# Projecting queries and keys of five heads in the first phase of an encoder layer

## The chip, the cores and the metric
The kernel runs on one core of a Trainium2 chip. The metric is the device time of one execution in microseconds (us); three runs of the kernel before gave 2012.86, 2015.05 and 2019.13 us, median 2015.05. All times below are from these runs or from one profiled execution.

## The reference
Two streams, 512 prompt frames and 64 sample frames (576 columns together, kept transposed: features on the partitions, frames along the free axis), go through two layers of width 2048. Layer A, which the change touches, is attention over chunks of 64 frames with a learned bias by relative distance:

```python
def a_project(h, w_in, g_q, g_k):
    q, k, v, g = jnp.split(h @ w_in, 4, axis=-1)
    return rmsnorm(q.reshape(hd), g_q), rmsnorm(k.reshape(hd), g_k), v.reshape(hd), g
...
sc = einsum('bqhd,bkhd->bhqk', q, kk) * A_SCALE + bias
p  = softmax(sc)
y  = x + (silu(g) * einsum('bhqk,bkhd->bqhd', p, vv)) @ w_out
```

with h = rmsnorm(x, ln), 16 heads of 128, so that `w_in` has 64 column blocks of 128: 16 of queries, 16 of keys, 16 of values, 16 of gates. Layer B is latent attention and is left as it is. All is in float32; a product is made of three matmuls on operands that are split into a high and a low part.

## The kernel before
Every operand x is split by `split` (L205, L206): ScalarE rounds it to a high part (named ...h), VectorE subtracts to get the low part (...l). `mm3` then issues high x high, high x low and low x high. A **direct projection** of one 128-wide block, `proj`, takes 16 x 3 x 2 = 96 matmuls of 288 columns. A **pair by block products**, `block_pairs`, makes two blocks together from seven products of half-size matrices, each of 24 matmuls of 288 columns: 168 in place of 192. It needs operands formed once from x (`block_operands`, tiles aiT4 to aiT7) and for every pair seven weight combinations, which `block_weights` adds on VectorE and splits (14 splits of 128 x 512, in place of 8).

PE's order is written out by the program: generators ("streams") run in `Order`, which keeps a planned time `od_.now`; a stream yields the planned time, the condition or the PSUM tag that it waits for, and the first ready stream of lowest rank issues next. The other engines' orders are set by the scheduler of the tile framework. PSUM has tags "mm" (2 buffers), "st" (1) and "x" (2).

Layer A goes in these stages:
- **First pass** (`values_and_gates`, L698): values 0, 1 and gates 0, 1 are projected together (tiles av, ag; 16 x 24 matmuls) while x is loaded. `stats_a` (tile lnast) sums the squares; from it comes `rs`, the row scale of the norm. Gates are copied out of PSUM (L716, L720); the two value results stay in the two "mm" buffers until `later` scales them by `rs` (L676) and gives "mm" back. Then value 2 and gate 2 are projected directly (tile ap) while the block operands are formed.
- **Block stage** (tiles ai35 to ai47): 13 pairs (value j, gate j), j = 3 to 15. Results go to DRAM through GpSimd's queue (`vT`, `vd`, `sgd`).
- **Heads** (`head_a`, L768): for head hd the query and key block are projected directly (tile a{hd}p). `qk_chain` copies the result out of PSUM (`raw_of`, L500), takes sums of squares (`halves`, L450 to L454, and a matmul a{hd}{0,1}st), scales (`rnorm`, L484 to L496) and splits into q and k operands. `v_chain` loads the value from `vd` (tile vt) and transposes it (vts, vtp). `attention` issues four score tiles and one for the sample (s0 to s3, s-1), transposed probabilities (t0 to t3, t-1) and the outputs (o-1, o3), in the order `ATT`; a score tile goes through softmax (L519 to L524) and back to PE as a transpose. While attention waits, PE takes matmuls of the next heads' projection: 192 per head.
- **Output projection**: the first two blocks (tile ao, `both`) run beside the last heads, as far as `heads_a` has split the heads' outputs (tiles oh, ol); block operands are formed from the outputs (L295); the rest are pairs (ao4 to ao14).

Of the kernel before, what the change touches and what calls it, by code (L numbers as in the profile page):

```python
# [20 lines left out]
P = 128  # L21
# [97 lines left out]
def encoder(tc, xT, wa_in, wa_out, wb_in, wuq, wuk, wuqr, wuv, wb_out, kcT, vc, ckvcT, krcT, gains, rtab,  # L119
# [25 lines left out]
    od = dram.tile([D, N], F32, name="od")  # L145
    vd = dram.tile([D, N], F32, name="vd")
    sgd = dram.tile([D, N], F32, name="sgd")
    qrd = dram.tile([D, N], F32, name="qrd")
    qd = dram.tile([D, N], F32, name="qd")

# [490 lines left out]

    ws = Weights(wload4, [(kt,) for kt in range(KT)], 2)
    h, xs = [], []
    state = {"ln": 0.0, "scored": -1, "in": False}

    def load_x(kt):
        x = tpx("x", F32, f"x{kt}")
# [36 lines left out]
        nc.gpsimd.dma_start(sgd[hd * P:(hd + 1) * P, :], y)  # L684

    def out_of(m, src, y):
        (value_of if m < MG else gate_a)(m, src, y)

    def y_tile(m):
        return tpy("y", F32, f"y{m}")  # L690

    def later(m, src, y, tag, n=1):
        yield lambda: state["ln"]
        out_of(m, src, y)
        if tag:
            od_.give(tag, L_M)

    def values_and_gates():  # L698
# [6 lines left out]
        for kt in range(KT):  # L705
            hi, lo = ws.get(3)
            for w in range(4):
                s = slice(w * P, (w + 1) * P)
                mm3(outs[w], (hi[:, s], lo[:, s]), [[x[:, c * 288:(c + 1) * 288] for x in h[kt]] for c in range(2)],
                    kt == 0, kt == KT - 1)  # L710
            yield None
            if kt + 4 < KT:
                load_x(kt + 4)
            square_sum(acc, xs[kt], tpx, N, kt == 0, f"lna{kt}")
        g1 = y_tile(MG + 1)
        ACT.copy(two(g1), pg1[:, :, :288])  # L716
        od_.give("st", L_M)
# [2 lines left out]
            ACT.copy(g0[:, c * 288:(c + 1) * 288], pg0[c][:, :288])  # L720
            od_.give("x", L_M)
        od_.spawn(1, stats_a(acc))
        for j in range(2):
            od_.spawn(1, later(MV + j, pv[j][:, :, :288], y_tile(MV + j), "mm"))
        od_.spawn(1, later(MG, two(g0), g0, None))
        od_.spawn(1, later(MG + 1, two(g1), g1, None))
        oX = Ahead((pair_x(j) for j in range(8)), 1)
# [8 lines left out]
        for _ in form:  # L736
# [1 line left out]
        close(g_x)  # L738
        g_w1, wp1 = pool("wblocks")
        pools.append(g_w1)  # L740
        yield from block_pairs(wa_in, X, [(MV + j, MG + j) for j in range(3, H)],
                               lambda name: wp1.tile([P, WH], F32, tag="o", bufs=10, name=name), None, y_tile,
                               lambda m, y: out_of(m, two(y), y), "ai")

# [18 lines left out]
        V.memset(t[:, :256], 0.0)  # L763
        nbA.append(t)
    o2 = [None] * H
    ws = Weights(wload, [p for hd in range(H) for w in range(2) for p in parts_of(wa_in, [w * H + hd], "wa")], 2)

    def head_a(hd):  # L768

# [2 lines left out]

        def qk_chain(which, ps):
            col = gak if which else gaq
            raw = raw_of(ps, tpa, N, f"{n_}raw{which}")
            if which:
                kc = ap_.tile([P, NC], F32, tag="kc", bufs=2, name=n_ + "kc")
                nc.sync.dma_start(kc, kcT[hd * P:(hd + 1) * P, :])
            yield lambda: state["ln"]
            st = yield from halves(raw, tpa, N, f"{n_}{which}")  # L780
            t0 = max(od_.now, state["ln"] - 2.0)
            z = rnorm(st, P, N, base=EX, coef=P * EPS / D)
            scaled(raw, col, z)
            yield lambda: state["scored"] >= hd - 1
            if which == 0:
                hi = ap_.tile([P, N], F32R, tag="qh", bufs=1, name=n_ + "qh")
                lo = ap_.tile([P, N], F32R, tag="ql", bufs=1, name=n_ + "ql")
                split(raw, hi, lo)
            else:
                nc.gpsimd.dma_start(kT[hd * P:(hd + 1) * P, :], raw)  # L790
                hi = ap_.tile([P, NK], F32R, tag="kh", bufs=1, name=n_ + "kh")
                lo = ap_.tile([P, NK], F32R, tag="kl", bufs=1, name=n_ + "kl")
                split(raw, hi[:, NC:], lo[:, NC:])
                split(kc, hi[:, :NC], lo[:, :NC])
            yield max(t0 + L_RN, od_.now + L_SP)
            got[which] = hi, lo

        def v_chain():
            vt = tpa("raw", F32, n_ + "vt")
            nc.gpsimd.dma_start(vt, vd[hd * P:(hd + 1) * P, :])  # L800
            vs = ap_.tile([P, 2, P], F32, tag="vs", bufs=2, name=n_ + "vs")
            nc.sync.dma_start(vs[:, 0, :], vc[hd * P:(hd + 1) * P, :])
# [11 lines left out]
            vl = ap_.tile([P, 512], F32R, tag="vl", bufs=1, name=n_ + "vl")  # L814
            split(tps, vh, vl)
            od_.give("x", L_T)
            got["v"] = vh, vl, vs

        sg = op_.tile([P, N], F32, tag="o", bufs=16, name=n_ + "sg")
# [2 lines left out]

        def bias():

            T = ap_.tile([P, 256], F32, tag="T", bufs=2, name=n_ + "T")
            nc.sync.dma_start(T, rtab[hd * P:(hd + 1) * P, :])
            nb = nbA[hd % 2]
            nbs = ap_.tile([P, PK], F32, tag="nbs", bufs=1, name=n_ + "nbs")
            V.tensor_scalar(out=nb[:, 256:], in0=T, scalar1=T[:, 0:1], scalar2=-1.0,
                            op0=ALU.subtract, op1=ALU.mult)  # L830
            V.tensor_copy(nbs, nb[:, 256:256 + PK])
            V.memset(nb[0:64, 448:], BIG)
            return nb, nbs
# [22 lines left out]

        od_.spawn(0, attend())
        for which in range(2):
            yield "mm"
            ps = ps_of("mm", f"{n_}p{which}")  # L860
            yield from proj(ps, ws, h, N)
            od_.spawn(1, qk_chain(which, ps))
        od_.spawn(1, v_chain())

# [471 lines left out]

L_VT, L_G, L_CQ, L_M, L_V, L_LN, L_HA, L_LB = 5.0, 5.8, 10.0, 1.5, 5.0, 5.0, 8.0, 4.0
ATT = "t0 s2 t1 s3 o-1 t2 t3"
DIRECT, GA, WRAW, WHL, SGB, DEEP, VA = 2, 2, 3, 5, 2, 2, 2
LAT = (0, 1, 2, 3, 8, 4, 5, 6, 7, 9, 10)  # L1340
LAHEAD = 1
# [85 lines left out]
```

## Time and profile before

| | |
|---|---|
| median of three runs | 2015.05 us (2012.86 to 2019.13) |
| profiled execution | 2007.77 us, its span 2005.9 us |
| TensorE (PE) busy | 1956.2 us, 98% of the span |
| VectorE (DVE) busy | 1491.2 us, 74% |
| ScalarE (ACT) busy | 1180.6 us, 59% |
| mean granted TensorE clock | 0.988 of 2.4 GHz |

Engines run at the same time, so their busy times don't add up to the span. A matmul's own duration is longer than its share of PE, since matmuls are pipelined: what one costs is the distance to the next start. "Idle before" in a row is the time that the engine stood still ahead of the instruction, with the instruction or DMA that ended it.

### The profile page before, as it was taken

What the parts mean: (1) busy time and instruction counts of PE and PEld (TensorE: products, weight loads), DVE (VectorE), ACT (ScalarE), POOL (GpSimd) and SP (SyncE); (2) the same over time, 40 slices, a digit from 0 to 9 for tenths busy, and PEclk for the clock granted to TensorE, in tenths of its full rate; (3) what the DMA queues carried; (4) which work ended last, traced back from release to release, by engine and by line L of the source; (5) the groups of instructions that cost most, each with busy time, mean ns of one, the idle gap of its engine ahead of it and who ended that gap; (6) DMA issues with size and microseconds to landing.
All of it is one profiled execution on the core that took longest, in us unless ns stands there. A gap on an engine that the chain in (4) does not pass through costs nothing.

```text
span 2005.9 us, 37809 instructions
## 1 busy us (share of the span) xinstructions
PE 1956.2 (98%) x14380; PEld 1932.3 (96%) x14380; DVE 1491.2 (74%) x2935; ACT 1180.6 (59%) x2214; POOL 136.9 (7%) x258
## 2 busy tenths in 40 slices
PE   8699999999999999999999899999999999999998
PEld 8699999999999999998999899999999999999998
DVE  8778888757777777779887648887776766776875
ACT  7655555556656565665544538986765666564332
POOL 1100000020000000000000200000000000002000
PEclk9899999999999999999999899999999999999999
DMA  7534444353222323222543525553222322256542
GB/s 232 190 117 135 141 133 134 120 198 92 91 91 88 98 81 99 84 92 66 190 148 108 182 80 147 161 165 117 78 84 88 91 86 83 83 153 222 168 143 64
DMA packets 125446, 247.00 MB, mean 123 GB/s; under 512 B 15808, under 2 KB 30160, under 8 KB 125264
## 3 DMA queue, kind: packets, MB, share of 16 engines
q1 hardware_dynamic: 104288, 171.46, 28.8%
q0 software_dynamic: 20976, 73.13, 10.5%
q8 instruction: 113, 1.85, 0.4%
q14 instruction: 69, 0.57, 0.1%
HBM read 198.07 MB, written 43.79 MB: 121 GB/s over the span
## 4 chain that ended last, share of the span: by engine, by line
PE 86%; issue 8%; DVE 2%; DMA 2%; ACT 1%; POOL 0%; SPq 0%; POOLq 0%; DVEq 0%; ACTq 0%
PE g L166 8%; PE lat L166 7%; PE u L166 4%; PE ao L166 2%; PE ap L166 1%; PE av L166 1%; PE a15p L166 1%; PE a14p L166 1%; PE a13p L166 1%; PE a12p L166 1%; PE a10p L166 1%; PE a9p L166 1%; PE a8p L166 1%; PE a7p L166 1%; PE a6p L166 1%
## 5 line engine op out<-in xcount | busy, mean ns | idle before, releaser
L206 DVE TENSOR_TENSOR wa_2l<-wa_2r,wa_2h 128x512 fp32r<-128x512 f32 x35 | 24.2, 691 | 19.7 <-ACT wa_2h L205 19.6
L205 ACT CAST wa_2h<-wa_2r 128x512 fp32r<-128x512 f32 x35 | 21.7, 620 | 21.4 <-PE a3p L166 1.9
L205 ACT CAST wa_0h<-wa_0r 128x512 fp32r<-128x512 f32 x35 | 21.5, 614 | 21.5 <-PE a0p L166 3.2
L206 DVE TENSOR_TENSOR wa_0l<-wa_0r,wa_0h 128x512 fp32r<-128x512 f32 x35 | 23.9, 684 | 11.7 <-ACT wa_0h L205 11.6
L206 DVE TENSOR_TENSOR wa_3l<-wa_3r,wa_3h 128x512 fp32r<-128x512 f32 x35 | 24.1, 687 | 11.1 <-ACT wa_3h L205 11.1
L206 DVE TENSOR_TENSOR wb_1l<-wb_1r,wb_1h 128x512 fp32r<-128x512 f32 x25 | 17.2, 688 | 15.0 <-ACT wb_1h L205 15.0
L166 PE MATMUL u<-cqh,wq_0h 128*128 128x288 f32 x128 | 27.7, 298 | 0.5 <-ACT q6raw L500 0.3
L205 ACT CAST wa_3h<-wa_3r 128x512 fp32r<-128x512 f32 x35 | 21.3, 609 | 10.4 <-PE a0p L166 4.4
L166 PE MATMUL u<-cqh,wq_0l 128*128 128x288 f32 x128 | 27.4, 296 | 0.0
L166 PE MATMUL u<-cql,wq_0h 128*128 128x288 f32 x128 | 27.3, 295 | 0.0
L206 DVE TENSOR_TENSOR wb_3l<-wb_3r,wb_3h 128x512 fp32r<-128x512 f32 x25 | 17.2, 687 | 13.2 <-ACT wb_3h L205 13.2
L166 PE MATMUL lat<-bh,wb_0h 128*128 128x288 f32 x88 | 19.9, 309 | 6.3 <-ACT bh L210 6.3
L205 ACT CAST wb_3h<-wb_3r 128x512 fp32r<-128x512 f32 x25 | 15.4, 616 | 17.8 <-PE lat L166 8.1
L205 ACT CAST wb_1h<-wb_1r 128x512 fp32r<-128x512 f32 x25 | 15.5, 618 | 17.5 <-PE lat L166 8.8
L206 DVE TENSOR_TENSOR wa_1l<-wa_1r,wa_1h 128x512 fp32r<-128x512 f32 x35 | 24.1, 689 | 2.0 <-ACT wa_1h L205 1.5
L166 PE MATMUL g<-bh,wb_1h 128*128 128x288 f32 x112 | 24.3, 298 | 0.0
L166 PE MATMUL g<-bh,wb_0h 128*128 128x288 f32 x112 | 24.3, 298 | 0.0
L166 PE MATMUL g<-bh,wb_2h 128*128 128x288 f32 x112 | 24.2, 298 | 0.0
L166 PE MATMUL g<-bh,wb_3h 128*128 128x288 f32 x112 | 24.2, 298 | 0.0
L166 PE MATMUL g<-bh,wb_0l 128*128 128x288 f32 x112 | 24.0, 296 | 0.0
L166 PE MATMUL g<-bh,wb_1l 128*128 128x288 f32 x112 | 24.0, 296 | 0.0
L166 PE MATMUL g<-bl,wb_1h 128*128 128x288 f32 x112 | 24.0, 296 | 0.0
(8217 smaller groups left out, 8616.4 us busy)
## 6 DMA issues: line engine op xcount, KB each, us to landing
wa_0r<-wa_in SPq DMA_DIRECT2D x34, 256.0 KB, 3.0
wa_1r<-wa_in SPq DMA_DIRECT2D x34, 256.0 KB, 3.1
wa_2r<-wa_in SPq DMA_DIRECT2D x34, 256.0 KB, 2.9
wa_3r<-wa_in SPq DMA_DIRECT2D x34, 256.0 KB, 3.0
wb_0r<-wb_in SPq DMA_DIRECT2D x25, 256.0 KB, 3.2
wb_1r<-wb_in SPq DMA_DIRECT2D x25, 256.0 KB, 3.2
wb_2r<-wb_in SPq DMA_DIRECT2D x25, 256.0 KB, 3.1
wb_3r<-wb_in SPq DMA_DIRECT2D x25, 256.0 KB, 2.9
```

The lines of the kernel that those rows point to most:

```text
L166: nc.tensor.matmul(out, lhs, rhs, start=start, stop=stop, **kw)
L205: ACT.copy(hi, src)
L206: V.tensor_tensor(out=lo, in0=src, in1=hi.bitcast(F32), op=ALU.subtract)
```

## The change
Heads 2, 5, 8, 11 and 14 (`EARLY`) get their query and key blocks as five more pairs at the end of the block stage. The raw results are stored to a new DRAM tensor `qkd`; `qk_chain` of these heads loads them into a tile of its own (`rawd`, two buffers) in place of copying from PSUM, and `head_a` projects nothing for them. At most two q/k chains and three raw tiles may be in work at once (`chains`, `raws`). The value tile `vt` has one buffer of its own, the bias tile `T` one in place of two. Value 0 of the first pass is copied out of PSUM by ScalarE straight after its last matmul, and its "mm" buffer is given back then.

```diff
+    qkd = dram.tile([2 * D, N], F32, name="qkd")
...
     def out_of(m, src, y):
-        (value_of if m < MG else gate_a)(m, src, y)
+        if m < MV:
+            nc.gpsimd.dma_start(qkd[m * P:(m + 1) * P, :], y)
+        else:
+            (value_of if m < MG else gate_a)(m, src, y)
...
+        v0 = y_tile(MV)
+        ACT.copy(two(v0), pv[0][:, :, :288])
+        od_.give("mm", L_M)
         g1 = y_tile(MG + 1)
...
-        for j in range(2):
-            od_.spawn(1, later(MV + j, pv[j][:, :, :288], y_tile(MV + j), "mm"))
+        od_.spawn(1, later(MV, two(v0), v0, None))
+        od_.spawn(1, later(MV + 1, pv[1][:, :, :288], y_tile(MV + 1), "mm"))
...
-        yield from block_pairs(wa_in, X, [(MV + j, MG + j) for j in range(3, H)],
+        yield from block_pairs(wa_in, X, [(MV + j, MG + j) for j in range(3, H)] + [(hd, H + hd) for hd in EARLY],
...
-    ws = Weights(wload, [p for hd in range(H) for w in range(2) for p in parts_of(wa_in, [w * H + hd], "wa")], 2)
+    ws = Weights(wload, [p for hd in range(H) if hd not in EARLY for w in range(2)
+                          for p in parts_of(wa_in, [w * H + hd], "wa")], 2)
...
-            raw = raw_of(ps, tpa, N, f"{n_}raw{which}")
+            if ps is None:
+                yield lambda: state["scored"] >= hd - 2
+                raw = ap_.tile([P, N], F32, tag="rawd", bufs=2, name=f"{n_}raw{which}")
+                r0 = (which * H + hd) * P
+                nc.gpsimd.dma_start(raw, qkd[r0:r0 + P, :])
+            else:
+                yield lambda: state["raws"] < 3
+                state["raws"] += 1
+                raw = raw_of(ps, tpa, N, f"{n_}raw{which}")
...
             yield lambda: state["ln"]
+            yield lambda: state["chains"] < 2
+            state["chains"] += 1
             st = yield from halves(raw, tpa, N, f"{n_}{which}")
...
             scaled(raw, col, z)
+            state["chains"] -= 1
...
+            if ps is not None:
+                state["raws"] -= 1
...
         def v_chain():
-            vt = tpa("raw", F32, n_ + "vt")
+            yield lambda: state["v"] >= hd - 1 and state["scored"] >= hd - 2
+            vt = ap_.tile([P, N], F32, tag="vt", bufs=1, name=n_ + "vt")
...
-            T = ap_.tile([P, 256], F32, tag="T", bufs=2, name=n_ + "T")
+            T = ap_.tile([P, 256], F32, tag="T", bufs=1, name=n_ + "T")
...
         for which in range(2):
-            yield "mm"
-            ps = ps_of("mm", f"{n_}p{which}")
-            yield from proj(ps, ws, h, N)
+            ps = None
+            if hd not in EARLY:
+                yield "mm"
+                ps = ps_of("mm", f"{n_}p{which}")
+                yield from proj(ps, ws, h, N)
             od_.spawn(1, qk_chain(which, ps))
...
+EARLY = 2, 5, 8, 11, 14
```

The change moves instructions on several engines (the changed file's lines of helpers stand one higher). Three places follow.

ScalarE at the end of the first pass, before (wa_3h is a weight split of the direct projection that comes next, aiT... block operands, xx reloaded x, y<-ag the copy of gate 1):

```order
L205 CAST wa_3h<-wa_3r 128x512
L205 CAST aiT5h_1131<-xx_1068 128x288
L205 CAST aiT7h_1141<-xx_1068 128x288
L661 ACTIVATE xx_1124<-xx_1124,gn 128x576
L205 CAST aiT6h_1137<-xx_1071 128x288
L205 CAST wa_0h<-wa_0r 128x512
L716 COPY y_761<-ag_171 128x576
```

and now (y<-av is the new copy of value 0):

```order
L206 CAST wa_3h<-wa_3r 128x512
L720 COPY y_762<-av_170 128x576
L206 CAST aiT5h_1133<-xx_1070 128x288
L662 ACTIVATE xx_1126<-xx_1126,gn 128x576
L206 CAST aiT6h_1139<-xx_1073 128x288
L206 CAST aiT7h_1143<-xx_1070 128x288
L206 CAST wa_0h<-wa_0r 128x512
L723 COPY y_764<-ag_172 128x576
```

The new copy stands right behind wa_3h, six instructions ahead of the copy of gate 1.

PE in head 14 before, ahead of the transpose of its first score tile (a15p is the projection of head 15, which fills the time since score tile 1):

```order
L166 MATMUL a15p_11123<-hh_439,wa_2l 128x288 x2
L166 MATMUL a15p_11123<-hh_479,wa_2h 128x288 x2
L166 MATMUL a15p_11123<-hl_480,wa_2h 128x288 x2
L166 MATMUL a15p_11123<-hh_479,wa_2l 128x288 x2
L166 MATMUL a15p_11123<-hh_519,wa_3h 128x288 x2
L166 MATMUL a15p_11123<-hl_520,wa_3h 128x288 x2
L166 MATMUL a15p_11123<-hh_519,wa_3l 128x288 x2
L166 MATMUL a15p_11123<-hh_559,wa_3h 128x288 x2
L166 MATMUL a15p_11123<-hl_560,wa_3h 128x288 x2
L166 MATMUL a15p_11123<-hh_559,wa_3l 128x288 x2
L170 MATMUL a14t_11272<-idt,a140P 128x128
L166 MATMUL a14s_11276<-a14kh,a14qh 128x384
```

and now, from the sample tile's transpose on:

```order
L171 MATMUL a14t-1_11682<-idt,a14sP 64x128
L167 MATMUL a14s_11688<-a14kh,a14qh 128x256
L167 MATMUL a14s_11688<-a14kl,a14qh 128x256
L167 MATMUL a14s_11688<-a14kh,a14ql 128x256
L171 MATMUL a14t_11698<-idt,a140P 128x128
L167 MATMUL a14s_11702<-a14kh,a14qh 128x384
L167 MATMUL a14s_11702<-a14kl,a14qh 128x384
L167 MATMUL a14s_11702<-a14kh,a14ql 128x384
L171 MATMUL a14t_11712<-idt,a141P 128x128 x2
L167 MATMUL a14s_11717<-a14kh,a14qh 128x512
```

The projection matmuls between score tiles and transposes are gone here: no head is left to project, and the output projection waits for heads.

DVE in head 14 now (a0sg to a13sg are finished heads' outputs, from which L296 forms block operands; L592 is the product of gate and output of head 13, the last row the softmax's first step on score tile 0):

```order
L592 TENSOR_TENSOR a13sg<-a13sg,a13o_11642 128x512
L296 TENSOR_TENSOR a10sg<-a10sg,a2sg 128x288
L296 TENSOR_TENSOR a3sg<-a3sg 128x288
L296 TENSOR_TENSOR a10sg<-a10sg 128x288
L207 TENSOR_TENSOR ol_11657<-a13sg,oh_11656 128x576
L296 TENSOR_TENSOR a3sg<-a11sg,a3sg 128x288
L296 TENSOR_TENSOR a4sg<-a4sg 128x288
L296 TENSOR_TENSOR a11sg<-a11sg,a3sg 128x288
L296 TENSOR_TENSOR a4sg<-a12sg,a4sg 128x288
L520 ISA a140P,a140sm<-a14s_11666,nbA_6173 128x128
```

Operand forming of the output stage stands between head 14's softmax steps; before, most of it stood in head 15.

## Rows read from the trace of the kernel before

**Rows 1.** Page, parts 1 and 2: busy times; PE and its clock in 40 slices.
```profile
PE 1956.2 (98%) x14380; PEld 1932.3 (96%) x14380; DVE 1491.2 (74%) x2935; ACT 1180.6 (59%) x2214; POOL 136.9 (7%) x258
...
PE   8699999999999999999999899999999999999998
...
PEclk9899999999999999999999899999999999999999
```
**Rows 2.** Timeline of PE after the first pass: start, us, instruction, idle before.
```profile
68.16 1.33 PE L166 MATMUL lnast<-lnas,ones 128*128 128x288 f32 x4 [7.86 <-ACT y L716]
...
76.81 0.85 PE L166 MATMUL ap<-hh,wa_0h 128*128 128x288 f32 x2 [7.31 <-DVE y L676]
```
**Rows 3.** Timeline of ACT at the same place.
```profile
64.63 0.60 ACT L205 CAST wa_3h<-wa_3r 128x512 fp32r<-128x512 f32 x1
...
67.48 0.63 ACT L716 COPY y<-ag 128x576 f32<-128x576 f32 x1
```
**Rows 4.** Windows by stage; columns in the first line.
```profile
core 0: us, PE busy (x) PEld busy (x) DVE busy (x) ACT busy (x) POOL busy (x), PEclk, DMA share, GB/s
60.31:76.81 16.50, 1.33 (x5) 0.99 (x5) 13.64 (x31) 12.28 (x26) 2.36 (x5) 0.59 0.53 167
76.81:104.23 27.42, 27.42 (x194) 27.42 (x195) 16.68 (x28) 10.87 (x19) 4.29 (x8) 0.94 0.59 200
329.80:352.01 22.21, 22.21 (x171) 22.21 (x170) 18.07 (x30) 12.20 (x23) 1.62 (x3) 1.00 0.42 136
...
583.44:616.26 32.82, 32.82 (x246) 32.42 (x246) 23.72 (x56) 19.99 (x42) 1.08 (x2) 1.00 0.30 91
898.50:931.14 32.64, 32.64 (x242) 31.99 (x242) 32.19 (x72) 24.10 (x50) 0.55 (x1) 1.00 0.22 67
931.14:951.48 20.34, 16.41 (x93) 13.72 (x91) 17.26 (x55) 7.84 (x22) 0.00 (x0) 0.81 0.20 61
```
**Rows 5.** Chain that ended last: start, us, pieces in head 6.
```profile
596.39 7.20 PE a6p L166 x54
```
**Rows 6.** Timeline of PE in head 1: wait for head 0's value.
```profile
426.53 0.27 PE L170 MATMUL a0vts<-idt,a0vt 128*64 128x128 f32 x1 [1.79 <-DMA a0vt<-vd]
```
**Rows 7.** Groups by line and form, DVE, heads 6 and 14: busy, mean ns, idle before.
```profile
L206 DVE TENSOR_TENSOR wa_2l<-wa_2r,wa_2h 128x512 fp32r<-128x512 f32 x2 | 1.4, 692 | 1.2 <-ACT wa_2h L205 1.2
...
L206 DVE TENSOR_TENSOR ol<-a14sg,oh 128x576 fp32r<-128x576 f32 x1 | 0.8, 751 | 0.0
```
**Rows 8.** Timeline of head 15, all engines: one softmax step.
```profile
936.30 0.28 PE L166 MATMUL a15s<-a15kh,a15ql 128*128 128x256 f32 x1
...
936.72 0.42 DVE L519 CUSTOM_DVE_ANT_0 a151P<-a15s,nbA 128x256 f32<-128x256 f32 x1
...
937.20 0.44 DVE L295 TENSOR_TENSOR a11sg<-a11sg,a3sg 128x288 f32<-128x288 f32 x1
937.56 0.44 DVE L295 TENSOR_TENSOR a4sg<-a12sg,a4sg 128x288 f32<-128x288 f32 x1
...
938.36 0.34 DVE L524 TENSOR_SCALAR a151P<-a151P,a151sm 128x256 f32<-128x256 f32 x1
```
**Rows 9.** Timeline of PE, end of head 15.
```profile
943.96 1.11 PE L170 MATMUL a15t<-idt,a153P 128*128 128x128 f32 x4 [0.41 <-DVE a153P L524]
945.75 0.80 PE L166 MATMUL a15o<-pth,a15vh 128*128 128x512 f32 x1 [0.68 <-ACT pth L205]
...
951.48 0.85 PE L166 MATMUL ao<-oh,wao_3h 128*128 128x288 f32 x2 [1.55 <-ACT oh L205]
```
**Rows 10.** DMA issues: count, KB each, median us to landing.
```profile
vd<-y POOLq DMA_DIRECT2D x16, 288.0 KB, 4.6
...
a5vt<-vd POOLq DMA_DIRECT2D x1, 288.0 KB, 3.2
```

More of the change, by code (lines that the diff above doesn't have):

```diff
@@ L643, in encoder @@
     h, xs = [], []
-    state = {"ln": 0.0, "scored": -1, "in": False}
+    state = {"ln": 0.0, "scored": -1, "in": False, "chains": 0, "raws": 0, "v": -1}
     def load_x(kt):
@@ L816, in v_chain @@
             od_.give("x", L_T)
+            state["v"] = hd
             got["v"] = vh, vl, vs
```

## The prediction
> **What bounds the kernel now.** I read the page first: PE is busy for 98% of the span, DVE for 74%, ACT for 59%, and the slices dip only at three seams [rows 1]. So time is PE's matmuls plus the places where PE stands. The windows by stage show the two stages that matter. In the heads PE is busy for all 32.82 us of a head while DVE works 23.72 [rows 4]. In the block stage a pair takes 22.21 us, all of it PE [rows 4]. The timeline of PE shows the largest wait: after the first pass it stands 7.86 us, does four matmuls, and stands 7.31 us more, until the values have been scaled and leave PSUM [rows 2].
>
> A matmul of 288 columns costs 7.20 / 54 = 0.1333 us [rows 5]. A head is then 192 x 0.1333 = 25.6 us of projection and 32.82 - 25.6 = 7.2 us of attention.
>
> **The sum is made against the profiled execution** (2007.77 us, span 2005.9) and carried over to the median of the runs, 2015.05, which is 7.3 us above it; I take the difference as the same for both kernels.
>
> **1. Five projections become five pairs.** 5 x (25.6 - 22.2) = 17.0 us off PE. The pairs I bound with the row of the present pairs: these have DVE busy 18.07 of 22.21 [rows 4], and the new ones have no gate to compute, so PE stays the limit there. Weight loads stay at eight blocks of 256 KB a head on SP's queue. On GpSimd's queue come ten stores and ten loads of 288 KB; such a store lands in about 4.6 us and such a load in 3.2 [rows 10], the loads are issued a head ahead or more, and DMA is at 0.30 in the heads: nothing. **-17.0**.
>
> **2. Value 0 leaves PSUM at once.** In ACT's order the new copy stands right behind the split of wa_3h, which ended at 64.63 + 0.60 = 65.2; with the 0.63 of such a copy [rows 3] the buffer is free at about 65.9, and the direct projection starts there instead of at 76.81 [rows 2]. The clock was at half level then as now (the window 60.31 to 76.81 has 0.59 [rows 4]), so that cost is the same. The statistic's four matmuls now come after 30 of the projection; its chain to the scaled values took 76.81 - 69.49 = 7.3 us and must end before the first of the two blocks is done, else PE waits for the second "mm" buffer. A clock of 0.94 over the 27.42 us of the projection now [rows 4] is 3.3 us at half level (0.06 / 0.5), 14 matmuls; so it reaches 30 at 65.9 + 3.3 + 16 x 0.1333 = 71.3, and the chain ends at 79 to 82 and the block at 80.8: about 1 us of wait. I take 10.9 - 1.4 = 9.5; the best is 10.6, and 6 if the chain, which shares ACT and DVE with the block operands, comes 4 us later. **-9.5**.
>
> **3. Head 0's value is loaded earlier** (its DMA now stands ahead of the gates' loads on GpSimd's queue): the 1.79 us wait goes [rows 6]. **-1.8**.
>
> **4. One buffer for vt and T.** The next value is loaded once the last was transposed. The nearest case is head 2: some 36 matmuls and a score tile, 6 us, lie between, against 3.2 us of landing [rows 10] and the issue. Nothing; at worst 2 us. A load of T holds the weight loads behind it on SP until the last bias was made, which in DVE's order lies ahead; three raw weight tiles cover it.
>
> **5. The heads lose their filler.** This is the term that decides. PE keeps 11 x 192 matmuls to fill 16 attentions. The new order spends about 150 a head in heads 2 to 10, enough to cover each wait, and has 72, 96, 96 and 12 (with the output projection's) in heads 11 to 14. From head 11's first score to head 15's first score PE needs 276 x 0.1333 + 4 x 7.2 - 2.1 (the output of head 14, which now stands behind) = 63.5 us.
>
> DVE needs more. A head's own DVE work is 23.72 less eight weight splits of 0.69 [rows 4, 7] = 18.2. In heads 11 to 14 the order has four of these less 21 rows of the q/k chains that now come earlier (0.67 each): 58.8; 11 weight splits of the output projection (7.6); 14 splits of heads' outputs at 0.75 [rows 7] (10.5); 26 forming steps at 0.45 (11.7) [rows 8]. Neighbours overlap, since two forming steps of 0.44 start 0.36 apart [rows 8]: 51 x 0.08 = 4 off. That is 84.6. The same reckoning gives head 14 of before 31.0, where the row has 32.19 [rows 4], so I go up a little, to 86. So heads 11 to 14 take 86 and not 63.5: +22.5. Head 15 in turn: it took 20.34 us with 48 filler matmuls [rows 4], that is 20.34 - 6.4 - 7.2 = 6.7 above its content; with 6 fillers every softmax step is bare. One step, from the end of the scores to P, took 936.4 to 938.7, 2.3 us [rows 8], and the last transpose to the restart of the output projection 7.5 [rows 9]. I take 8.7 above content: +2. Together **+24.5**. Below: if DVE didn't matter, four bare heads would still hold 2.3 us steps that PE can't fill, about +12. Above: if PE and DVE also wait for each other in turn, +33.
>
> The Trainium skill has a sentence that speaks against this edit ("Perfetto Trace Analysis", Matmul Optimizations): matmul speed is scaled with utilization, so matmuls should come back to back in batches. The trace agrees: granted clock 0.81 in head 15's window [rows 4], where fillers run out. By it the bare heads 14 and 15 would run their 14.4 us of attention at the 1.2 GHz level, up to 14 us more, most of it under DVE's time.
>
> **6. Heads 0 to 10** hold DVE busier: 18.2 and six weight splits (22.3 us) to 150 matmuls and 7.2 (27.2 us) is 82% instead of 72, and near 95 in heads 0 and 1, where the order has three heads' chains at once. In head 14 of before DVE was busy 32.19 of 32.64 and PE never waited [rows 4], so I take little: **+2**, 0 to 10.
>
> Sum: -17.0 - 9.5 - 1.8 + 24.5 + 2 = -1.8 us, that is 2013.2. A change of under 0.3% (6 us) can't be told from none.
>
> **The rivals.**
> *Faster: the tail is cheap.* All but terms 5 and 6 give -28.3. If DVE's extra rows slip into gaps, term 5 is near +12: -14, 2001. For it: PE did not wait in head 14 before, at 99% DVE. Against it: there 32 us of PE work covered those 32 us of DVE, and now PE's content is less than DVE's. The extreme of it follows from a rule of the Trainium skill ("Perfetto Trace Analysis", Identifying the Most-Contended Engine): performance comes from the engine of highest occupancy, to be improved first. Taken by PE's 98% alone, nothing is lost in the heads and the time is 2015.05 - 28.3 = 1986.8. The row of head 14, where DVE has 99%, says that in this stretch the engine is another. I give this extreme 0.05 of the faster chance.
>
> *Slower: the bare tail pays twice.* In heads 11 to 15 PE waits for a softmax step, DVE then waits for PE's transpose, and the granted clock falls to the half level, as its 0.81 in head 15 shows for part of that window [rows 4]; then term 5 is 33 and more, term 6 up to 10, and the sum is +15: 2030. It decides from terms 5 and 6 together above 34.3. For it: every row of the order in head 14 depends on the row before. Against it: the scheduler puts softmax ahead of other DVE work.
>
> *The copy of value 0 does nothing*, as ACT stands in front of it for a load of x, or the second buffer is awaited in full: term 2 is -3, the sum +5: no change, still within the forecast.
>
> **Chances.** With terms 5 and 6 together below 22.3 it is faster by more than 6 us, above 34.3 slower; I expect 26.5 of 12 to 43. No change 0.40, faster 0.34, slower 0.26. The likeliest case's own range is 2009 to 2021; 2000 to 2028 takes in both neighbours but for the far ends.
>
> **What would show it.** Ap starting near 66 us and ai35 near 95; five pairs of 22.2 us; heads 2 to 10 at 24 to 29 us with PE full; then heads 11 to 14 with DVE full and PE waiting for DVE rows, some 23 us in all, and clock 0.5 in heads 14 and 15. Wrong would be: PE full up to head 14, or PE waits spread over heads 0 to 10, or DVE idle in the tail.

## The result and the profile after

The changed kernel is slower: median 2041.47 us (2038.77 to 2043.47) against 2013.95 (2012.54 to 2019.13) for the kernel before; the ratio is 1.0131, with a 95% interval of 1.0109 to 1.0153. Forecast were 2013.2 us and "no change", with a range of 2000 to 2028. The profiled execution after took 2041.44 us, its span 2039.7. The profiled execution of before (2007.77) lies 6.2 us under its median, so the two spans differ by 33.8 us where the medians differ by 27.5; the account below is of the spans.

The page after, parts 1 and 2 (answering to [rows 1]):

```profile
PE 1961.4 (96%) x14260; PEld 1927.0 (94%) x14260; DVE 1538.5 (75%) x3020; ACT 1199.4 (59%) x2255; POOL 147.9 (7%) x278
...
PE   8899999999999999987999899999999999999998
...
PEclk9899999999999999988899999999999999999999
```

PE has 120 recorded matmuls fewer and yet 5 us more busy time. It has gaps in slices 18 and 19, 867 to 969 us, and slices 18 to 20 have a lower clock: they hold heads 11 to 15.

**The first pass** went nearly as forecast. PE's timeline after (start, us, instruction, idle before; compare [rows 2]):

```profile
67.03 0.85 PE L167 MATMUL ap<-hh,wa_0h 128*128 128x288 f32 x2 [7.12 <-ACT y L720]
...
73.61 0.70 PE L167 MATMUL lnast<-lnas,ones 128*128 128x288 f32 x4
...
96.01 0.29 PE L167 MATMUL ai35a<-hh,ai35p10h 128*128 128x288 f32 x1
```

The direct projection starts at 67.0 in place of 76.8, the first pair at 96.0 in place of 104.1. Then a little is given back; waits of PE in the first pass and the block stage after (line waited, what for: us, times, longest):

```profile
PE ap L167 <- ACT y L720: 7.1, 1, 7.1
PE ai35a L167 <- DVE y L414: 1.7, 1, 1.7
PE ai35a L167 <- ACT y L412: 0.6, 1, 0.6
```

The first pair stands 2.3 us for its results, which go into tiles y. There are four of these, and the copied value now holds one: VectorE, ahead of scaling value 2 into a tile y, stands until a store from such a tile has landed, where it didn't wait before (start, us, instruction, idle before):

```profile
90.08 0.76 DVE L677 TENSOR_TENSOR y<-ap,rs 128x576 f32<-128x576 f32 x1 [3.30 <-DMA vd<-y]
```

That the 2.3 us come from this wait alone is not shown. The last value pair starts at 365.6 against 370.9: 5.3 us are kept.

**The heads.** Windows after, cut at each head's first score tile s0 (heads 0, 1, 4, 8, then 11 to 15, the last up to the restart of the output projection; columns as in [rows 4]):

```profile
547.80:576.10 28.30, 28.30 (x213) 27.89 (x212) 25.07 (x60) 23.00 (x47) 1.09 (x2) 1.00 0.27 84
576.10:603.00 26.90, 25.05 (x183) 24.20 (x183) 23.26 (x57) 18.58 (x41) 1.62 (x3) 1.00 0.36 112
...
658.20:689.40 31.20, 29.01 (x204) 28.38 (x203) 26.49 (x61) 20.57 (x42) 2.70 (x5) 0.95 0.36 116
...
774.40:806.00 31.60, 29.02 (x204) 28.26 (x203) 20.28 (x50) 20.14 (x41) 0.54 (x1) 0.95 0.22 68
...
863.90:892.30 28.40, 21.85 (x132) 19.72 (x131) 22.07 (x53) 21.31 (x43) 0.54 (x1) 0.82 0.16 48
892.30:919.40 27.10, 22.40 (x150) 20.86 (x149) 25.94 (x61) 21.01 (x44) 1.08 (x2) 0.94 0.23 71
919.40:944.10 24.70, 19.81 (x137) 18.06 (x136) 23.92 (x65) 13.09 (x30) 1.63 (x3) 1.00 0.26 82
944.10:962.00 17.90, 13.10 (x55) 10.12 (x55) 12.72 (x43) 7.04 (x19) 0.71 (x1) 0.66 0.05 16
962.00:981.27 19.27, 13.55 (x54) 9.66 (x52) 10.72 (x33) 7.42 (x20) 0.00 (x0) 0.68 0.03 5
```

From head 11 on neither PE nor DVE is full, and the clock is lower in four of the five heads.

**What PE's work alone would take** can be worked out: the filler matmuls (288 columns each, of the next heads' projections and of the first output blocks) that PE takes between two first score tiles, by 0.1333 us, and 7.2 us of attention a head. This sum I call **the content**. Before, heads 0 to 10 have 2082 fillers, so 277.5 + 79.2 = 356.7 us, and heads 11 to 14 have 762, so 130.4. The two stretches of the trace of before are:

```profile
443.70:800.70 357.00, 357.00 (x2656) 352.62 (x2655) 259.95 (x604) 219.67 (x450) 11.89 (x22) 1.00 0.30 91
800.70:931.50 130.80, 130.80 (x973) 128.96 (x972) 104.56 (x239) 84.86 (x174) 3.79 (x7) 1.00 0.27 83
```

So the reckoning holds within 0.4 us. After, they have 1662 and 264 fillers: 300.7 and 64.0 us. The trace after:

```profile
547.80:863.90 316.10, 306.90 (x2238) 300.41 (x2236) 256.23 (x604) 213.29 (x443) 16.24 (x30) 0.99 0.31 96
863.90:962.00 98.10, 77.17 (x468) 68.76 (x467) 84.65 (x218) 62.44 (x134) 3.95 (x7) 0.87 0.18 57
```

What a stretch takes beyond its content I call **the loss**: 15.4 us in heads 0 to 10 and 34.1 in heads 11 to 14; before, 0.3 and 0.4. Heads 11 to 14 have 78, 96, 84 and 6 fillers and lose 10.8, 7.1, 6.2 and 10.0 us. Head 15 loses 19.3 - 7.2 - 0.8 = 11.3, before 6.4.

| part | us |
|---|---|
| first pair starts earlier, less what the block stage gave back | -5.2 |
| ten projections gone (960 x 0.1333), five pairs added (111.0) | -17.0 |
| ahead of the first score (50.6 to 48.9) | -1.7 |
| loss in heads 0 to 10 | +15.1 |
| loss in heads 11 to 14 | +33.7 |
| loss in head 15 | +4.9 |
| behind the restart of the output projection | +4.0 |
| sum (spans: 33.8) | +33.8 |

The last row is in stages that the change doesn't touch. That stretch took 1054.4 us before and 1058.4 after, but 1054.1 in run 6, which has the same early heads: it varies between executions, and I don't count it as an effect of the change. Its cause is open.

**How the tail loses.** The chain that ended last, after, at the start of head 11 (start, us, pieces):

```profile
866.29 0.42 DVE a111P L520
866.73 0.21 DVE a110P L525
...
867.07 0.30 PE a11t L171
867.37 0.54 PE a11s L167 x3
867.93 0.56 DVE a112P L520
868.50 0.28 DVE a111P L525
...
868.91 0.66 PE a11t L171 x2
...
872.62 0.53 ACT a13raw L501
...
873.20 3.25 PE a15p L167 x12
```

Within 7 us the end passes from DVE to PE, back to DVE, to PE, ACT and PE: each waits for another. PE stands from 870.85 to 873.20 while DVE and ACT are both busy; over heads 11 to 14 none of the three is busy throughout. The last row shows the second price: 12 fillers took 3.25 us, 0.27 each, where they take 0.133 at full clock [rows 5]. Windows of the same stretch, and of a wait in head 4:

```profile
655.00:660.40 5.40, 5.40 (x43) 5.20 (x41) 5.34 (x16) 3.17 (x8) 0.00 (x0) 1.00 0.01 2
660.40:662.60 2.20, 0.04 (x1) 0.01 (x1) 1.63 (x4) 2.17 (x5) 0.00 (x0) 1.00 0.35 115
662.60:664.60 2.00, 1.98 (x11) 1.95 (x11) 2.00 (x3) 0.99 (x2) 0.00 (x0) 0.63 0.45 142
664.60:666.60 2.00, 2.00 (x11) 2.00 (x10) 1.08 (x5) 1.63 (x4) 0.54 (x1) 0.52 0.29 110
666.60:668.60 2.00, 2.00 (x17) 2.00 (x17) 1.77 (x5) 1.86 (x5) 0.00 (x0) 1.00 0.10 39
...
870.85:873.20 2.35, 0.00 (x2) 0.01 (x1) 2.31 (x7) 2.35 (x7) 0.00 (x0) 0.50 0.00 0
873.20:877.00 3.80, 3.80 (x16) 3.78 (x17) 1.51 (x4) 2.43 (x4) 0.00 (x0) 0.50 0.19 52
```

PE stands 2.2 us, and for the next 4 us it runs mostly at the 1.2 GHz level (granted clock 0.63 and 0.52), with 11 matmuls in 2 us where it has 17 at full clock. In heads 11 to 14 PE stood 98.1 - 77.2 = 20.9 us. By the profile's list of waits some 8 of them were for softmax rows and 7.5 for the q/k chains (statistics, and PSUM tiles that a raw copy frees); the rest were for values and for splits of outputs. The clocks 0.82, 0.94, 1.00 and 0.66 of the four heads are (28.4 x 0.18 + 27.1 x 0.06 + 17.9 x 0.34) / 0.5 = 25.7 us at half level, which cost up to half of that, 12.8. The two make at most 33.7 us, about the loss of 34.1; how it divides between them is not measured. Standing doesn't always lower the clock: in head 13 PE stood 4.9 of 24.7 us at 1.00.

**The theory after the result:** projection matmuls were PE's cover, work that it could do while it waited for softmax steps and chains; without them PE stands, and its clock falls (heads 11 to 15); in heads 0 to 10 the q/k chains of early heads run beside others', and PE's order reaches their tiles too early. **The rival** is the prediction's own: VectorE's throughput holds the tail.

### The profile page after: what moved, and what is told of

Its sections match the earlier page's. It is cut to its first block, busy times and chain, and to the rows that moved or that the text cites. A ratio compares the mean times of both kernels' runs of the same rounds, so it can differ in the third digit from the quotient of the medians.

```text
span 2039.7 us, 37808 instructions
## 1 busy us (share of the span) xinstructions
PE 1961.4 (96%) x14260; PEld 1927.0 (94%) x14260; DVE 1538.5 (75%) x3020; ACT 1199.4 (59%) x2255; POOL 147.9 (7%) x278
## 4 chain that ended last, share of the span: by engine, by line
PE 76%; issue 9%; DVE 5%; ACT 3%; DMA 2%; POOL 0%; SPq 0%; POOLq 0%; DVEq 0%; ACTq 0%
PE g L167 8%; PE lat L167 6%; PE u L167 3%; PE ao L167 1%; PE a7p L167 1%; PE a12p L167 1%; PE a9p L167 1%; PE a4p L167 1%; PE a0p L167 1%; PE a1p L167 1%; PE a10p L167 1%; PE a13p L167 1%; PE a15p L167 1%; PE a6p L167 1%; PE a3p L167 1%
## 5 line engine op out<-in xcount | busy, mean ns | idle before, releaser
L167 PE MATMUL u<-cqh,wq_0h 128*128 128x288 f32 x128 | 27.6, 298 | 0.5 <-ACT q6raw L501 0.3
L207 DVE TENSOR_TENSOR wb_3l<-wb_3r,wb_3h 128x512 fp32r<-128x512 f32 x25 | 17.2, 687 | 14.3 <-ACT wb_3h L206 14.1
L206 ACT CAST wb_3h<-wb_3r 128x512 fp32r<-128x512 f32 x25 | 15.4, 616 | 18.4 <-PE lat L167 9.1
L206 ACT CAST wa_0h<-wa_0r 128x512 fp32r<-128x512 f32 x25 | 15.4, 615 | 15.6 <-DMA wa_0r<-wa_in 7.2
L207 DVE TENSOR_TENSOR wb_2l<-wb_2r,wb_2h 128x512 fp32r<-128x512 f32 x25 | 17.1, 685 | 9.7 <-ACT wb_2h L206 9.7
L167 PE MATMUL g<-bh,wb_3l 128*128 128x288 f32 x112 | 24.0, 295 | 0.0
L167 PE MATMUL g<-bl,wb_3h 128*128 128x288 f32 x112 | 24.0, 296 | 0.0
L167 PE MATMUL g<-bl,wb_2h 128*128 128x288 f32 x112 | 24.0, 296 | 0.0
L167 PE MATMUL g<-bh,wb_2l 128*128 128x288 f32 x112 | 24.0, 295 | 0.0
L167 PE MATMUL g<-bl,wb_0h 128*128 128x288 f32 x112 | 23.9, 295 | 0.0
```

The source lines that it names most:

```text
L167: nc.tensor.matmul(out, lhs, rhs, start=start, stop=stop, **kw)
L206: ACT.copy(hi, src)
L207: V.tensor_tensor(out=lo, in0=src, in1=hi.bitcast(F32), op=ALU.subtract)
```

## The experiments

Each is compared with the kernel before in its own group of runs (median 2011.45 us for the first four, 2011.93 and 2011.95 for the next two groups). "Loss" is worked out as above.

**1. The copy of value 0 alone**, in the kernel before:

```diff
+        v0 = y_tile(MV)
+        ACT.copy(two(v0), pv[0][:, :, :288])
+        od_.give("mm", L_M)
...
-        for j in range(2):
-            od_.spawn(1, later(MV + j, pv[j][:, :, :288], y_tile(MV + j), "mm"))
+        od_.spawn(1, later(MV, two(v0), v0, None))
+        od_.spawn(1, later(MV + 1, pv[1][:, :, :288], y_tile(MV + 1), "mm"))
```

> The kernel before with value 0 copied out of PSUM at once, and nothing else of the change: heads 2, 5, 8, 11, 14 keep their projections, all buffers as before. Theory (the early copy is a clean gain, the loss is all in the heads): the first pair starts at 96 us in place of 104.2, 1.7 + 0.6 us of it are given back as waits in that pair, and the heads are as before: -5.5 to -9.5 us against before. Rival (the copy only moves the wait into the block stage, or the heads give it back): within 2 us of before.

Measured: 2005.15 us, ratio 0.9956 (0.9942 to 0.9970), 6 to 12 us. The first pair started at 95.4, with waits of 1.5 + 1.4 us, the last value pair at 365.7, and the heads took 357.1 and 130.7 us. The copy is a clean gain, its cost in the block stage included. The wait for head 0's value (1.79 us [rows 6]) was 3.2 us here, since its load still stands behind the gates'.

**2. All of the change but the early heads:**

```diff
-EARLY = 2, 5, 8, 11, 14
+EARLY = ()
```

> The changed kernel with no early head: the early copy of value 0, the limits on chains and raw tiles and the single vt and T buffers stay, the five pairs and the loads of raw results go. The order of fillers is that of before (192 a head). Theory (limits and buffers cost nothing by themselves): as the copy alone, less the 1.8 us of head 0's value, so -7 to -11 us against before, heads at 32.8 us with PE full. Rival (the limits and single buffers make PE wait in the heads): heads of 33.5 us and more, 0 to +15 us against before.

Measured: 2000.77 us, ratio 0.9937 (0.9922 to 0.9952): 10 to 16 us faster than before. Heads 0 to 14 in the trace:

```profile
437.60:794.70 357.10, 357.10 (x2656) 352.73 (x2655) 259.96 (x604) 219.68 (x450) 11.89 (x22) 1.00 0.32 91
794.70:925.50 130.80, 130.80 (x973) 128.98 (x972) 104.57 (x239) 84.84 (x174) 3.79 (x7) 1.00 0.30 84
```

PE is full, and the loss is that of before. The limits and single buffers cost nothing with this order of fillers, and head 0's value is no longer waited for. **This version beats both kernels**; of those tried it is the fastest.

**3. The change without the copy of value 0:**

```diff
-        v0 = y_tile(MV)
-        ACT.copy(two(v0), pv[0][:, :, :288])
-        od_.give("mm", L_M)
```

> The changed kernel without the early copy of value 0: the five early heads with all their buffers and limits. Theory: the two parts add up, so it stands above the changed kernel by what the copy alone gains, 5.5 to 9.5 us: 2047 to 2051 us, +33 to +37 against before. Rival (the copy is given back in the changed kernel): 2040 to 2043 us.

Measured: 2050.46 us, ratio 1.0181 (1.0161 to 1.0200). In the traces the first pair starts 9.9 us later than with the copy (105.9 to 96.0), and the span is 7.7 us longer. With the first pass as in the kernel before, the first pair starts 1.8 us later here than in the profiled execution of before (104.1), which was thus on the quick side. The parts add up, and the median lies in the theory's range; the loss in the heads is nearly the same (15.1 and 35.6).

**4. The early heads elsewhere**, with the same work on each engine:

```diff
-EARLY = 2, 5, 8, 11, 14
+EARLY = 0, 3, 6, 9, 12
```

> The changed kernel with heads 0, 3, 6, 9, 12 early in place of 2, 5, 8, 11, 14: the same PE, DVE and ACT work, but PE's order has 138, 150, 96 and 108 filler matmuls in heads 11 to 14 in place of 72, 96, 96 and 12; the projection ahead of head 0 falls from 354 matmuls to 198. Theory (heads 11 to 15 lose because PE has too few matmuls beside softmax and the clock falls): the tail from head 11's first score to the output projection's restart, less its PE content, falls from about 35 us to 15 to 20, heads 0 to 10 lose the same 19 us, and the total is 2021 to 2029 us. Rival A (DVE's work sets the time of the heads wherever the fillers are): 2037 to 2044 us, DVE over 95% in the tail. Rival B (head 0 early exposes its load from DRAM and its chain at the start): above 2041 us.

Measured: 2017.71 us, ratio 1.0029 (1.0019 to 1.0038), some 21 us better than the change against its own runs of before, and below what was expected. Its two stretches (1602 and 480 fillers, content 292.7 and 92.8 us):

```profile
533.20:837.30 304.10, 295.19 (x2173) 288.82 (x2172) 251.41 (x597) 209.92 (x437) 14.97 (x28) 1.00 0.32 96
837.30:938.50 101.20, 94.38 (x686) 91.00 (x685) 89.90 (x223) 66.60 (x144) 4.53 (x8) 1.00 0.28 82
```

The tail's loss falls from 34.1 to 8.4 us, that of heads 0 to 10 from 15.4 to 11.4, at clock 1.00. DVE does more in the tail than in the changed kernel (89.9 us to 84.7), in a stretch 3 us longer that holds 29 us more of PE's work. With the same work, where the fillers stand decides. Head 0 early costs 5 us in front of the first score, as rival B had it, but not more than is gained.

**5. More matmuls for the tail**, of no use:

```diff
                 ps = ps_of("mm", f"{n_}p{which}")
+                if hd == 15:
+                    for j in range(DUMMY // 2):
+                        x = h[KT - 1][0]
+                        matmul(ps[:, j % 2, :288], x[:, :P], x[:, :288], True, True)
+                        if j % 6 == 5:
+                            yield None
                 yield from proj(ps, ws, h, N)
...
+DUMMY = 324
```

> The changed kernel with 324 more matmuls of 288 columns on PE, ahead of head 15's projection and into the same PSUM tile, which the projection then overwrites: heads 11 to 14 have 162, 156, 150 and 132 fillers in place of 72, 96, 96 and 12. They read only operands that are there and feed nothing; by 0.1333 us each they are 43.2 us of PE work. Theory (the tail's loss is PE standing still and running at half clock for want of work beside softmax): they fall into time that was lost anyway, the clock is 1.0 up to head 14, heads 11 to 14 take their PE content of 107 us and up to 5 more where they took 98.1, and the total rises by 9 to 15 us only: 2050 to 2056. Rival (the tail is held by waits in PE's order that fillers don't cover): all 43 us are added, 2080 and more. A third way (DVE's rows hold the tail at 98 us whatever PE does): at most +9 with DVE over 95% busy in heads 11 to 14.

Measured: 2051.24 us, ratio 1.0199 (1.0181 to 1.0217), 9.8 us above the changed kernel (spans: 10.3) for 43.2 us of added work. Heads 11 to 14 (588 fillers, content 107.2):

```profile
865.60:976.10 110.50, 107.52 (x793) 105.09 (x792) 89.44 (x225) 64.27 (x138) 3.79 (x7) 1.00 0.20 58
```

The clock is 1.00, the loss 3.3 us. Three quarters of work that serves nothing cost no time: that much of the tail was PE standing or running at half clock. The rule of the Trainium skill that the prediction weighed ("Perfetto Trace Analysis", Matmul Optimizations) reads "The matmul engine dynamically scales power based on utilization, so it's important that matmuls execute back-to-back in batches": it speaks of power, not of speed as the prediction has it. The trace agrees with its advice: heads 11 to 14 ran at 0.87 without the added matmuls and at 1.00 with them.

**6. Later planned times for the q/k chains**, in the changed kernel:

```diff
-        yield od_.now + L_HA
+        yield od_.now + wait
...
-        od_.give("st", L_ST)
+        od_.give("st", held)
...
-        od_.give("mm", L_M)
+        od_.give("mm", held)
...
-                raw = raw_of(ps, tpa, N, f"{n_}raw{which}")
+                raw = raw_of(ps, tpa, N, f"{n_}raw{which}", 4.0)
...
-            st = yield from halves(raw, tpa, N, f"{n_}{which}")
+            st = yield from halves(raw, tpa, N, f"{n_}{which}", 11.0)
...
-            z = rnorm(st, P, N, base=EX, coef=P * EPS / D)
+            z = rnorm(st, P, N, base=EX, coef=P * EPS / D, held=7.0)
```

In the changed kernel these are the waits of PE in the heads that it is aimed at:

```profile
PE a12p L167 <- ACT a10raw L501: 2.6, 1, 2.6
PE a15p L167 <- ACT a13raw L501: 2.3, 1, 2.3
PE a60st L167 <- DVE a51sq L490: 2.2, 1, 2.2
PE a121st L167 <- DVE a111sq L490: 1.6, 1, 1.6
```

The third is the wait of head 4 shown above: the statistic of head 6 needs the one st buffer, which the chain of head 5, an early head, still holds.

> The changed kernel with other planned times for the q/k chains of the heads, which only move where PE takes their matmuls: the statistic's matmul 11 us after the chain's start in place of 8, its PSUM tile given back after 7 us in place of 4, a projection's PSUM tile given back 4 us after its copy in place of 1.5. Theory (in heads 0 to 10 PE loses because two chains run at once and PE's order reaches st and mm before ScalarE and VectorE are done): some 10 us of waits for st and raw copies shrink, heads 1, 4 and 8 take 27 to 29 us in place of 26.9, 31.2 and 31.6, total 2029 to 2036 us. Rival (the chains are late whatever PE does; the wait moves to the scores): 2038 to 2045 us.

Measured: 2025.41 us, ratio 1.0065 (1.0045 to 1.0085), below both ranges. The profiled execution, 2020.95 us, was the quickest of the four. Content 294.3 and 67.2 us:

```profile
549.30:849.80 300.50, 297.65 (x2190) 292.43 (x2189) 251.07 (x600) 211.43 (x439) 16.25 (x30) 0.99 0.33 99
849.80:945.60 95.80, 80.62 (x491) 72.63 (x491) 85.03 (x216) 62.44 (x137) 3.96 (x7) 0.88 0.20 62
```

The loss of heads 0 to 10 falls from 15.4 to 6.2 us, and no wait for st is left among the longer ones. Heads 1 and 4 take 24.7 and 27.6 us and lose next to nothing; head 8 takes 25.6, but with 102 fillers in place of 150, and still loses 4.8. So 9 of the 15 us were the order, not the engines. The tail loses 28.6, some 5 less than without the later times.

**7. Both at once**, early heads 0, 3, 6, 9, 12 with the planned times of run 6 (edit as in 4 and 6).

> The kernel with heads 0, 3, 6, 9, 12 early and the later planned times of the run beside it. Theory: the spread of fillers and the waits for st and mm are two separate losses, so this gains 4 to 10 us on the even spread alone: 2008 to 2014 us. Rival: no gain, 2015 to 2020 us.

Measured: 2022.10 us, ratio 1.0051 (1.0035 to 1.0066): no gain on run 4, and above the rival's range too. Heads 0 to 10 lose 9.2 in place of 11.4, 6.2 of it in head 0 alone, but heads 11 to 14 lose 14.3 in place of 8.4. The later times let PE take 60 more fillers ahead of the first score (258 to 198), and heads 11 to 14 have 456 in place of 480; heads 12 and 13, with 102 and 96, lose 5.3 and 7.4. The supply is fixed: what is spent early is missing late.

**8. Three early heads, spread so that none runs dry:**

```diff
-EARLY = 2, 5, 8, 11, 14
+EARLY = 3, 7, 11
```

> The changed kernel with three early heads, 3, 7 and 11: no head from 0 to 14 has fewer than 120 fillers, and the output projection keeps its 258. Theory (a head with 120 fillers or more loses nothing but some 4 us where an early head's two chains run beside another's): from the run with no early head (2000.8) 3 x 3.4 us are saved and 3 x 4 lost, 1998 to 2006 us, clock 1.0 in all heads but 15. Rival A (the loss of the changed kernel is the same for each early head, 47 us over five): 2023 to 2029 us. Rival B (the loss is all starvation, which this spread avoids): 1989 to 1993 us.

Measured: 2018.38 us, ratio 1.0036 (1.0023 to 1.0050), far above what I expected, and between the ranges of the theory and of rival A. Content 303.1 and 109.6 us:

```profile
504.20:829.40 325.20, 310.32 (x2253) 303.56 (x2252) 257.81 (x602) 214.23 (x442) 14.08 (x26) 0.98 0.30 91
829.40:938.80 109.40, 109.40 (x813) 107.86 (x812) 91.77 (x219) 72.99 (x155) 3.80 (x7) 1.00 0.28 83
```

The tail with 606 fillers loses nothing, as the theory has it. Heads 0 to 10 lose 22.1 us, 7 for each early head and not the 4 I had read from heads 1, 4 and 8 of the changed kernel. Fillers alone don't save a head: head 1 has 204 and loses 5.5. The longest waits are again for st (3.4, 2.9 and 2.6 us).

**9. The same three with the planned times of run 6** (edit as in 6 and 8).

> Heads 3, 7 and 11 early, with the later planned times for the q/k chains (statistic's matmul 11 us after the chain's start, st held 7 us, a projection's tile 4 us). With the planned times of the change, this spread lost 24 us in heads 0 to 10 with 120 fillers and more in each, and nothing in heads 11 to 14. Theory (that loss is PE's order reaching st and scores before two chains that run at once are done): about half of it goes, 2003 to 2010 us. Rival (the load of the raw results or the work of three chains itself is late): 2015 to 2020 us.

Measured: 2004.45 us, ratio 0.9968 (0.9956 to 0.9980), in the theory's range. The loss of heads 0 to 10 falls from 22.1 us (the 24 in the expectation is too high) to 9.5: more than half of it was PE's order. Of the rest, PE stands idle 6.6 us in head 2 alone (25.15 busy of 31.70 us), though it has 126 fillers there and VectorE is busy for 23.67 us only. The two longest waits:

```profile
PE a2s L167 <- DVE ptl L207: 2.9, 2, 1.7
PE a2s L167 <- DVE a2pts L561: 1.5, 1, 1.5
```

These are score tiles of head 2 that wait for VectorE to take the head's own transposed probabilities out of PSUM: neither st nor the loads. Head 0 of runs 7 and 12 loses its 6 us at rows of the same kind. That PE's order comes too early here too is likely, but no run moved these tiles.

**10. Less work for VectorE in the tail**, in the changed kernel:

```diff
+                if j in LEAVE:
+                    ACT.copy(hi, oA[j])
+                    o2[j] = hi, hi
+                    continue
                 lo = t1.tile([P, N], F32R, tag="hl", bufs=32, name=f"ol{j}")
...
+        ACT.copy(hi, raw)
+        return hi, hi
...
-    wo = Weights(wload, two_first(parts_of(wa_out, range(4), "wao")), 3)
+    wo = Weights(wload_high, two_first(parts_of(wa_out, range(4), "wao")), 3)
...
+LEAVE = range(14)
```

> The changed kernel without VectorE's low parts of heads' outputs 0 to 13 and of the first two output blocks' weights (the high part is used in their place, so the output product is computed on coarser operands): 14 rows of 0.75 and 11 of 0.68 us go from VectorE in heads 11 to 14, 18 of its 84.7 us; PE's order is unchanged. Theory (PE, ScalarE and VectorE wait for each other in turn, and PE has too little beside it): only rows that stood in front of a softmax row matter, heads 11 to 14 take 90 to 96 us in place of 98.1. Rival (VectorE's throughput holds the tail, as the prediction had it): 80 to 84 us.

The kernel leaves out the low parts. As the high part is put in their place, high x high is counted three times, which is more than the coarser operands that the expectation names: the outputs are not those of the layer. PE's matmuls in heads 11 to 14 are the same in number.

Measured once: 2040.64 us. Heads 11 to 14:

```profile
863.00:963.50 100.50, 80.21 (x468) 72.81 (x467) 72.96 (x196) 61.55 (x134) 3.80 (x7) 0.85 0.19 56
```

VectorE works 73.0 us in place of 84.7 (11.7 less, where 18 were expected), and the stretch takes 100.5 in place of 98.1. Not even the 2 to 8 us that my theory allowed were gained. The rival falls: VectorE's throughput doesn't hold the tail. Nor do softmax rows that stand in line behind other rows on VectorE: from each reciprocal (L524) to the product that follows it (L525), the 16 softmax steps of these heads wait 11.7 us in all in the changed kernel and 4.4 here, without a gain.

**11. One early head, head 0:**

```diff
-EARLY = 2, 5, 8, 11, 14
+EARLY = 0,
```

> One early head, head 0: its chains run beside the projections of heads 1 and 2 ahead of the first score, all later heads keep 174 to 198 fillers. Theory (an early head costs only where chains bunch or fillers run out, and this one meets neither): 3.4 us under the run with no early head (2000.8), less up to 3 us for the wait on head 0's value: 1996 to 2001 us. Rival (every early head costs 5 us and more net): 2006 us or more.

Measured: 2006.51 us, ratio 0.9980 (0.9969 to 0.9991), 5.7 us above the run with no early head (spans: 4.9): not what I expected, and the rival's number. The heads lose nothing (352.1 and 130.8 us against 351.9 and 130.4 of content). But the stretch ahead of the first score takes 35.5 us for 198 fillers (26.4), a loss of 9.1 against 1.4 in run 2, largely since PE stands for head 0's own statistics. So the cost stands where head 0's chains run; whether every early head costs as much, as the rival has it, this run can't show. Waits of PE up to there, the two that matter:

```profile
PE a00st L167 <- DVE a00s L455: 4.1, 1, 4.1
...
PE a01st L167 <- DVE a00sq L490: 1.4, 1, 1.4
```

**12. The same with later planned times** (edit as in 6 and 11).

> The same with the later planned times. Theory: PE is full in these heads either way, so within 3 us of the run beside it; rival: 54 fillers more stand ahead of the first score, so the last heads miss them and it is 3 to 8 us slower.

Measured: 2012.94 us, ratio 1.0005 (0.9996 to 1.0014), 6.4 above run 11, the rival's size. Its reason holds in small part: 60 more fillers stand ahead of the first score, which comes 7.6 us later, and heads 11 to 14 have 24 fewer and lose 1.6 in place of 0.4. But heads 0 to 10 lose 6.4 us in place of 0.2, 6.1 of it in head 0, which has 132 fillers and waits as head 2 in run 9.

## Why the prediction was wrong

Point by point, by its own numbers:

- **Term 1, -17.0: right.** The five pairs took 22.2 us each (111.0), the 960 matmuls taken out are worth 0.1333 each; the sum of the spans closes with both.
- **Term 2, -9.5: right in kind, its size open.** The copy did what was said: ap started at 67.0 (66 forecast), the first pair at 96.0 (95). The block stage gave back 2.9 us, which no bound held: I had costed the new tile y at nothing, and VectorE then waits for one. The traces thus show -5.2, below the worst case of 6; the runs of experiment 1 give 6 to 12. Part of the difference is the quick first pass in the profiled execution of before (run 3).
- **Terms 3 and 4, -1.8 and 0: right** (-1.7; run 2 shows the single buffers at nothing).
- **Term 5, +24.5 (12 to 33): the step that failed.** "DVE needs more" was the step: DVE's rows in heads 11 to 14 were put at 84.6 us and are 84.65, yet that is not what the heads take. They took 98.1, with DVE at 86% and PE at 79%, and run 10 shows that 11.7 us less of DVE's work save nothing. That the rows' sum came out to the tenth doesn't speak for the step. I took the larger of two engines' sums for the time of a stretch; that holds while one of them has work ready throughout, as PE had before. Here both wait in turn, and the clock falls besides. Head 15 lost 4.9 more than before, not 2. Together 33.7 + 4.9 = 38.6, above the upper bound.
- **Term 6, +2 (0 to 10): failed as well.** "In head 14 of before DVE was busy 32.19 of 32.64 and PE never waited, so I take little." That head had 186 fillers and one head's chains at a time. With early heads the chains run beside others', and PE's order reaches the st buffer and the "mm" buffers before they are free; the heads lost 15.1 us more. Runs 6 and 9 take 9 and 13 us of such loss away by planned times alone; what the remainder hangs on is open (run 9's trace points to the score tiles).
- **Small slips, none of which decides:** 3.3 us at half level hold 12 matmuls of 0.267 us, not 14; the last score matmul of [rows 8] ends at 936.58, so the softmax step took 2.1 us, not 2.3; and the order's 276 fillers in heads 11 to 14 (72, 96, 96 and 12) are 264 in the trace (78, 96, 84 and 6).

**The rival "bare tail pays twice" was the mechanism in the main**: waits in turn, and the half clock. What it doesn't name are the q/k chains, for which PE stood about a third of its 20.9 us. Its point of decision was terms 5 and 6 above 34.3; they came to 53.7. I gave it 0.26 and priced its end at +15, as I took its worst cases (33 and 10) from rows in which PE still had cover. The sentence against it, that the scheduler puts softmax ahead of other DVE work, was about DVE's queue and says nothing of a chain that passes through three engines.

The rule on the most-contended engine (the Trainium skill, "Perfetto Trace Analysis", Identifying the Most-Contended Engine: "Optimize this engine first"), taken by PE's busy share, would have given 1986.8. The section itself wants TensorE judged by MFU (its useful arithmetic as a share of the peak) and by the busy share of its weight loads, not by matmul busy time. The weight loads' 96% [rows 1] name the same engine. In the tail no engine is that: PE was busy for 79% of heads 11 to 14, VectorE 86, ScalarE 64, and the trace speaks against the rule there.

Of "what would show it", ap, ai35 and the pairs came true; PE's waits in heads 11 to 14 were 20.9 us (some 23 forecast), but DVE was not full there, heads 4 and 8 took over 31 us (24 to 29 forecast), and the clock in heads 14 and 15 was 0.66 and 0.68, not 0.5. Of "wrong would be", two came true: PE waits in heads 0 to 10, and DVE idle in the tail.

## What to carry to other kernels

Work that fills another stage's waits can be worth up to its full length there: making it cheaper elsewhere (25.6 to 22.2 us a head) saves the 3.4, and takes away 25.6 us of cover. Before moving it, divide the fillers that are left by the heads: in this kernel most heads with 132 or more lost next to nothing, and the five of the change with 6 to 96 lost 38.6 us more than before. The count isn't enough by itself: where PE's order reached a tile before the engines were done with it, heads with 132 and 204 fillers lost 6.1 and 5.5 us (head 0 of run 12, head 1 of run 8). And the larger of two engines' busy sums is a lower bound of a stretch, not its time: follow the chain through the engines at the place that loses its cover.

## What the runs showed of the hardware

A wait of 2.2 us of PE was followed by 4 us of mostly half clock (0.63 and 0.52), (2 x 0.37 + 2 x 0.48) / 0.5 = 3.4 us of it, so that it cost up to 1.7 us beyond its own length; in heads 11 to 14 the clock's part was at most 13 of 34 us. And 43.2 us of matmuls that serve nothing lengthened the kernel by only 10 (run 5): where PE would stand or run at half clock, three quarters of the added work were free.
